# Attention values projected with tokens on partitions, in a hybrid decoder layer on one core

## The chip, the cores and the metric

The program runs on one core of a Trainium2 chip. The metric is the device time of one execution in microseconds; less is better. Three runs of the kernel before took 854.75, 854.88 and 855.74 us, median 854.88.

## The reference

One layer of a decoder over 256 prompt tokens and 8 requests with 8 new tokens each (64 sample tokens, 320 in all). Everything is float32. The residual stream (320 x 2048) goes through one wide projection whose columns feed three branches; the part that matters here is the sparse attention:

```python
z = jnp.einsum('btd,dn->btn', h, w)              # 2048 -> 8272 columns
aq, ak, av, ag, iq, ik, iw, bq, bf, bi, bg, mq, mg = jnp.split(z, cuts, axis=-1)
sc = sum_h iw[h] * relu(iq[h] . ik)              # 16 index heads of 64
sel = top_k(sc, 64 for the prompt, 256 for a sample request)
p = softmax(aq . ak[sel] / sqrt(128));  a_out = p @ av[sel]     # 8 heads of 128
```

A sample request attends over 2048 cached keys and values, which lie in 16 pages of 128 tokens, named by a page table, and over its 8 new ones. The second branch is a gated linear recurrence (HGRN2, 4 heads), the third attends to 256 memory tokens. Each branch is multiplied by a gate, the three are concatenated, projected by `w_out` and normalised. New keys, values, index keys and states are outputs too.

## The kernel before

**Precision.** The fast format of TensorE (`F32R`) holds a rounded float32, so each large product is made in three passes: a tensor is split into a high part and a rest (`xh`, `xl` for the tokens, `wh`, `wl` for a weight), and `xh*wh + xl*wh + xh*wl` is accumulated in PSUM.

**Projection.** The input projection goes column block by column block in the order of `PROJECTIONS`: first the index keys and two index heads, then `queries` (index and attention queries), `ak`, `av`, and then HGRN and gates, with the memory's projection between. For nearly all of it the weights are stationary: a 128 x 128 piece of the weights is loaded and the 320 tokens stream past, so the result has its features on partitions and the tokens along the row (tile `pj`, two PSUM banks that alternate). An entry of `wspec` is one 512 KB load of weights (ring `wr`, 3 buffers), prepared in two halves by a cast on ScalarE (`wh`) and a subtraction on VectorE or GpSimd (`wl`); `pe_quantum` runs an entry in four quanta of 6 products. When a block has all of its 16 slices, its evacuation stands in `pending` until PSUM holds the result and tiles of ring `t` are free. `ev_ak` turns a head of keys by the rotary tables (a shuffle and a product on VectorE read the bank); `ev_av` copies a head of values, 128 features x 320 tokens, and stores it to `vT`.

**Attention values.** The product of probabilities and values needs tokens on partitions. `attn_values` therefore transposes each head on TensorE: three transposes of 128 columns, a copy to `avn` (prompt) and one to `avS` (the 64 sample tokens), then three products with the transposed probabilities `probs(h)`. `attn_scores` makes those: scores, exponent and division in two `t` tiles `P0`, `P1`, three transposes, and a copy into space of `cat` that is free at that time.

**Pages.** Keys and values of the cache come in units: for a pair of requests and two pages each, 4 loads of 512 KB (`load_pages`, queue of SP). Tags `pg` (5 buffers) and `S` (3) hold them. A key unit is 16 products of 32 stationary columns by 256, a value unit 8 by 512, spread over the four 32-column groups of TensorE, so that four run side by side. Units go in the order of `PAGES` and, where both are loaded, two at a time; a key unit needs the queries, a value unit the softmax `soft(p)` of its pair, which needs the mask of the sample's top-k.

**Order.** All engines run their instructions in order, and one program writes that order out ahead of time. `Plan` keeps an estimated clock for every engine, with a price for each operation (`Engine.cost`), a time for each transfer and a time from which each tile can be read. The main loop at the end moves with TensorE: it starts loads (`loads`), prepares weights, issues evacuations, resumes the generators in `bg` (`background`) whose wants are met, and then gives TensorE a unit if `units_now` says so, or the next quantum if `half_ready` says so; if neither is ready, the estimated time moves on. After a unit, `join_visit` may add work that asked for a shared visit (`need(..., visit=...)`): such work waits up to `visit` us of the plan for one before it goes alone. The plan decides the order only; on the chip semaphores do.

**Other names.** `idx_load` brings the index keys, 32 KB pieces through GpSimd's indirect loads and SP, into a tile of 128 x 2048 for each pair of requests (`st["ci", p]`); `idx_sample` scores them; `idxdone` marks its end and is followed by `topk_sample`, 32 rounds of an 8-fold maximum and a replacement on VectorE. `masks` brings constants. Ring `bp` has two tiles of 4 KB a partition, shared by the index queries, the constants, the top-k's running count, HGRN and the memory queries (`pad_queries`). `VACC` is the sum of a pair's value units in PSUM bank `va`. `new_keys(p)` makes the scores of a pair against the new keys.

Of the kernel before, what the change touches and what calls it, by code (L numbers as in the profile page):

```python
# [47 lines left out]
IDLE = 3.0  # L48
LOOK = 3
# [96 lines left out]
class Engine:  # L146
# [41 lines left out]
    def cost(self, op, outs, ins, n):  # L188
        if self.name == "PE":
# [8 lines left out]
            if a.dtype == F32R:  # L198
                return turn + 0.0087 + n * 0.0004325
# [29 lines left out]
def hymba_step(ctx: ExitStack, tc: tile.TileContext, I, O):  # L229
# [223 lines left out]
    def pad_queries():  # L453
        yield from wait(("mq", 0))
# [70 lines left out]
    def add_block(kind, i):  # L525
# [3 lines left out]
        elif kind == "mem":  # L529
            for k in range(16):  # L530
                wspec.append(dict(kind="mem", k=k, n=1024, nq=2, src=I["wm"][:, k, :]))
        else:
            base, ev = {"iq": (32, ev_iq), "aq": (0, ev_aq), "ak": (8, ev_ak), "av": (16, ev_av), "mq": (56, ev_mq),
# [128 lines left out]
    def page_tag(n):  # L662
# [3 lines left out]
        if (len(PG) - len(in_s) + ("q" in st) + ("more" in st) + ci_live(0) < BUFS["pg"]  # L666
                and plan.slot_free("pg", BUFS["pg"]) <= plan.now + 0.2):
            return "pg"
# [53 lines left out]
    def unit(n):  # L722
# [21 lines left out]
        elif kind == "V":  # L744
            if u == 0:
                VACC[p] = PS([128, 512], "va")
            for j in range(2):
# [31 lines left out]
    def unit_ready(n):  # L779
        kind, p, u = punits[n]  # L780
        if any((n, b) not in PG or plan.avail(PG[n, b]) > plan.now for b in range(2)):
            return False
# [4 lines left out]
        if kind == "V":  # L787
            return ("soft", p) in done and plan.avail(PTt[p]) <= plan.now and (u < 7 or "attn" in done) and (
# [8 lines left out]
    def loaded(n):  # L797
        return all((n, b) in PG and plan.avail(PG[n, b]) <= plan.now for b in range(2))
# [38 lines left out]
    def ci_live(k):  # L837
        return sum([0, 1, 1, 1][p] == k and ("ci", p) in st for p in range(4))

    def idx_load():  # L840
# [3 lines left out]
        for sp in range(2):  # L844
            for p in (2 * sp, 2 * sp + 1):
                st["ci", p] = x = new([128, PAST], "S" if p else "pg")
                plan.pinned.add(x.tensor.name)
                plan.split.add(x.tensor.name)
            for c in range(2):
                for f in (1, 0):  # L850
                    for p in (2 * sp, 2 * sp + 1):
                        parts = []
                        j = 8 * f + 4 * c
# [6 lines left out]
                        for i in range(2):  # L860
                            x = st["ci", p][:, 128 * (j + i):128 * (j + i) + 128]
# [3 lines left out]
                        for i in range(2, 4):  # L865
                            for b in range(2):
                                yield from idle("SP", 0.5)
                                x = st["ci", p][64 * b:64 * b + 64, 128 * (j + i):128 * (j + i) + 128]
# [48 lines left out]
    def idx_sample():  # L917
# [77 lines left out]
        def stack(k):  # L995

            sp, c, f, a = steps[k]
            raw = st["ci", 2 * sp + a][:, 1024 * f + 512 * c:1024 * f + 512 * c + 512]
# [5 lines left out]
            if (c, f) == (1, 0):  # L1004
                plan.pinned.discard(st["ci", 2 * sp + a].tensor.name)
                del st["ci", 2 * sp + a]
# [142 lines left out]
    def attn_scores():  # L1149
        yield from wait("pbias", "idxdone")  # L1150
        for h in range(8):
            yield from wait(("aq", h), ("ak", h))
            yield from room(2)
# [4 lines left out]
            P0, P1, s8 = T(128), T(256), T8()  # L1158
# [17 lines left out]
            ACT.copy(probs(h), pt)  # L1176
            free(P0, P1)
            done.add(("probs", h))

    def attn_values():  # L1180
        for h in range(8):
            yield from wait(("probs", h), ("av", h))
            yield need(AV[h])
            avn = new([128, 2, 128], "avn")
            ps = PS([128, 3, 128])
            for i in range(2):
                PE.transpose(ps[:, i, :], AV[h][:, 128 * i:128 * i + 128], ident)
            PE.transpose(ps[:, 2, :], AV[h][:, 192:320], ident)
            ACT.copy(avn, ps[:, 0:2, :])
            ACT.copy(avS[64:128, 128 * h:128 * h + 128], ps[64:128, 2, :])  # L1190
            free(AV.pop(h))
            pts = probs(h)
            yield need(pts, avn)
            po = PS([128, 256])
            PE.matmul(po[:, 0:128], avn[:, 0, :], pts[:, 0:128], start=True, stop=True)
            PE.matmul(po[:, 128:256], avn[:, 0, :], pts[:, 128:256], start=True, stop=False)
            PE.matmul(po[:, 128:256], avn[:, 1, :], pts[:, 256:384], start=False, stop=True)
            cat_put(h, "p", slice(0, 256), po, ACT.copy)
        done.add("attn")

    def new_keys(p):
# [4 lines left out]
        yield need(akS, st["qpad"], visit=VISIT_WAIT)  # L1206
# [55 lines left out]
    def extract(p):  # L1262
# [3 lines left out]
        for i in range(2):  # L1266
            ACT.activation(o[i], VACC[p][:, 256 * i:256 * i + 256], AF.Copy, scale=RS[p][:, 1:2])
        del VACC[p], PTt[p]
# [96 lines left out]
    def hgrn():  # L1365
        lb, olb = lbt[:, 8:12], lbt[:, 12:16]
        yield from wait("idxdone", "pbias", "masks")
        for h in range(4):
# [4 lines left out]
            late_q = new([128, 2, 48], "kN")  # L1373
            yield from room(2, spare=spare)
# [270 lines left out]
    def half_ready(i, q):  # L1645
# [40 lines left out]
    def pe_quantum(i, q):  # L1686
# [12 lines left out]
        if s["kind"] == "T":  # L1699
# [14 lines left out]
            if s["k0"] + s["nk"] == 16 and last:  # L1714
                pending.append((s["evac"], pj.pop(s["evac"]), 3))
                if i == last_T:
                    done.add("lastT")
        elif s["kind"] == "mem":
# [86 lines left out]
    def ln_load(m):  # L1805
# [8 lines left out]
        if m == 0:  # L1814
            x = new([128, 2, 8, 6], "avn")
# [171 lines left out]
    def masks():  # L1987
        yield from wait("idxdone")
        yield from room(2, "bp")
        cm = [new([128, 1024], "bp"), new([128, 1024], "bp")]  # L1990
        SP.dma_start(lbt[:, 0:8], I["lb"])
        SP.dma_start(ngt, I["ng"])
        SP.dma_start(cm[0], I["cm"][:, 0:1024])
        SP.dma_start(cm[1], I["cm"][:, 1024:2048])
        yield need(*cm, lbt, ngt)
        ACT.copy(cu8, cm[0][:, 0:304])
# [275 lines left out]
```

## Time and profile before

| | |
|---|---|
| median of three runs | 854.88 us (854.75 to 855.74) |
| profiled execution | 854.57 us, span 852.8 us |
| TensorE busy, products | 843.1 us |
| weight loads of TensorE | 718.0 us |
| VectorE, ScalarE, GpSimd busy | 553.9, 422.3, 326.0 us |
| moved by DMA | 266.49 MB, mean 312 GB/s |

The span runs from the first instruction to the last; the profiled execution's own time has 1.8 us around it. TensorE's products are pipelined: one is still running when the next starts, so a row's duration is longer than its share of the engine, and what a product costs in a stream is the distance between starts. Nearly every operation has line 157, the helper that records all of them; rows are told apart by their tiles, output to the left of the arrow: `pj<-xh,wh` is a product of the input projection, `kv<-pg,qpad` one of a key unit, `va<-pg,PT` one of a value unit, `mB<-ident,t` a transpose. A product of true float32 operands stands as two records.

### The profile page before, as it was taken

To read this page: it belongs to the slowest core of one execution; us is meant where nothing else is said; L and a number is where in the kernel's file an instruction comes from. 1 tells how busy PE (TensorE), PEld (TensorE's weight loads), DVE (VectorE), ACT (ScalarE), POOL (GpSimd) and SP (SyncE) were. 2 spreads that over 40 slices of the span, in tenths; PEclk is the share of its full clock that TensorE was granted. 3 is DMA by queue.
4 is the path that set the end of the run, shared out by engine and by line. 5 is a ranking of instruction groups with operands and counts; after the bars stand their busy time and mean duration, and the time that the engine had idled before them with its cause. 6 is when DMAs were issued, how large, how long until landed. Compare 5 with 4: busy or idle time off the path is not lost.

```text
span 852.8 us, 19150 instructions
## 1 busy us (share of the span) xinstructions
PE 843.1 (99%) x6892; PEld 718.0 (84%) x6892; DVE 553.9 (65%) x1100; ACT 422.3 (50%) x908; POOL 326.0 (38%) x333
## 2 busy tenths in 40 slices
PE   9999999999999999999999999999999999999996
PEld 8999999877889898878778788787887889888885
DVE  7788897744897898654474556557545343953655
ACT  6454565553555543634544554554444353744432
POOL 0677562564634445331142214333311110714424
PEclk9999999999999999999999999999999999999998
DMA  9567456889999999999989999999999988756633
GB/s 342 172 189 228 156 172 251 279 307 411 376 389 397 335 327 359 398 360 403 389 330 409 408 353 389 401 397 377 347 409 400 364 324 291 272 171 199 195 99 123
DMA packets 83216, 266.49 MB, mean 312 GB/s; under 512 B 10481, under 2 KB 21170, under 8 KB 82482
## 3 DMA queue, kind: packets, MB, share of 16 engines
q1 hardware_dynamic: 82098, 263.18, 83.6%
q0 software_dynamic: 1024, 2.10, 0.8%
q8 instruction: 54, 0.88, 0.4%
q14 instruction: 40, 0.33, 0.1%
HBM read 256.50 MB, written 8.73 MB: 311 GB/s over the span
## 4 chain that ended last, share of the span: by engine, by line
PE 98%; DMA 1%; DVE 0%; SPq 0%; ACT 0%; DVEq 0%; issue 0%
PE pj L157 57%; PE mB L157 13%; PE va L157 10%; PE mA L157 10%; PE kv L157 8%; DMA S<-in_first 1%; DVE pg L157 0%; SPq L157 0%; ACT xh L157 0%; ACT PT L157 0%; DVE s L157 0%; DVEq L2258 0%; DVE avn L157 0%
## 5 line engine op out<-in xcount | busy, mean ns | idle before, releaser
L157 ACT CAST wh<-wr 128x512 fp32r<-128x512 f32 x334 | 205.0, 621 | 243.5 <-PE pj L157 183.9
L157 PE MATMUL pj<-xh,wh 128*128 128x320 f32 (+1 forms) x992 | 313.6, 316 | 0.0
L157 PE MATMUL pj<-xh,wl 128*128 128x320 f32 (+1 forms) x992 | 303.9, 306 | 0.0
L157 PE MATMUL pj<-xl,wh 128*128 128x320 f32 (+1 forms) x992 | 303.8, 306 | 0.0
L157 DVE TENSOR_TENSOR wl<-wr,wh 128x512 fp32r<-128x512 f32 x222 | 172.7, 785 | 181.9 <-ACT wh L157 166.5
L157 POOL TENSOR_TENSOR wl<-wr,wh 128x512 fp32r<-128x512 f32 x112 | 151.0, 1357 | 240.2 <-ACT wh L157 222.7
L157 PEld LDWEIGHTS pj<-xh,wh 128*128 128x128 f32 x992 | 186.7, 188 | 16.0 <-issue 12.5
L157 PEld LDWEIGHTS pj<-xl,wh 128*128 128x128 f32 x992 | 186.8, 188 | 1.3
L157 PEld LDWEIGHTS pj<-xh,wl 128*128 128x128 f32 x992 | 186.6, 188 | 0.0
L157 POOL TENSOR_TENSOR t<-t,t 128x256 f32<-128x256 f32 (+3 forms) x53 | 46.2, 873 | 119.5 <-ACT t L157 60.0
L157 PE MATMUL va<-pg,PT 128*32 128x512 f32 x456 | 58.4, 595 | 0.0
L157 PE MATMUL kv<-pg,qpad 128*32 128x256 f32 (+1 forms) x916 | 57.5, 380 | 0.0
L157 PEld LDWEIGHTS kv<-pg,qpad 128*32 128x32 f32 (+1 forms) x916 | 30.8, 110 | 20.4 <-issue 1.3
L157 PEld LDWEIGHTS va<-pg,PT 128*32 128x32 f32 x456 | 14.6, 109 | 30.4 <-issue 28.1
L157 DVE MAX8 PT<-PT 128x8 f32<-128x1032 f32 x32 | 39.5, 1234 | 0.5
L157 DVE MATCH_REPLACE8 PT<-PT 128x1032 f32<-128x1032 f32 x32 | 39.0, 1218 | 0.0
L157 POOL DMA_INDIRECT S<-in_ci,row x24 | 25.5, 1064 | 20.0 <-DVE row L157 10.6
L157 PE MATMUL mB<-t,wh 128*128 128x256 f32 x128 | 24.5, 289 | 0.0
L157 POOL TENSOR_TENSOR bp<-t,bp 128x128 f32<-128x128 f32 (+1 forms) x17 | 10.7, 627 | 36.0 <-ACT bp L157 36.0
L157 DVE TENSOR_TENSOR cat<-S,cat 64x512 fp32r<-64x512 f32 x24 | 19.5, 813 | 6.9 <-ACT cat L157 6.4
L157 POOL TENSOR_TENSOR t<-t,tabm 128x320 f32<-128x320 f32 x16 | 14.5, 908 | 24.4 <-DVE t L157 24.2
L157 POOL TENSOR_TENSOR xl<-cat,xh 128x256 fp32r<-128x256 f32 x12 | 12.5, 1061 | 24.8 <-ACT xh L157 24.8
(430 smaller groups left out, 1355.0 us busy)
## 6 DMA issues: line engine op xcount, KB each, us to landing
wr<-in_wt SPq DMA_DIRECT2D x124, 512.0 KB
pg<-in_ck SPq DMA_DIRECT2D x114, 512.0 KB
pg<-in_cv SPq DMA_DIRECT2D x114, 512.0 KB
wr<-in_wo SPq DMA_DIRECT2D x36, 512.0 KB
wr<-in_wm SPq DMA_DIRECT2D x16, 512.0 KB
S<-in_ck SPq DMA_DIRECT2D x14, 512.0 KB
S<-in_cv SPq DMA_DIRECT2D x14, 512.0 KB
pg<-in_cXV SPq DMA_DIRECT2D x8, 512.0 KB
```

What stands on the lines that cost most here:

```text
L157: res = f(*a, **k)
```

## The change

1. **Values with tokens on partitions.** The block `av` becomes 16 entries of kind `av`: two chunks of 512 columns, each over 8 loads of two slices. The tokens are stationary: 128 prompt tokens (`m` 0), 128 more (`m` 1), and, for `m` 2, the sample tokens' high and low parts side by side in one 128-wide weight `xS`, which `sample_columns` copies together into both `bp` tiles after `idxdone`. 512 columns of weights stream past; three passes for `m` 0 and 1, two for `m` 2. The accumulators are both `pj` banks and `va`; a chunk starts when nothing is pending and one `pj` bank and `va` are free. `ev_av` copies, adds the two halves of the sample part into `avS`, and stores rows of tokens (output `v`). `attn_values` has no transposes left.
2. **Scores in place.** `attn_scores` writes its probabilities to `probs(h)` at once, without two `t` tiles and without waiting for room for them.
3. **Value units** wait for the sample values of both chunks, since `va` is shared, and `VACC` is pinned until it is read.
4. **Index keys** lie by halves of the pages, a tile for each half of two pairs, and a tile is given back after its half.
5. **Pages** are requested from entry 28 on (38 before), and a unit counts as loaded 2 us of the plan after its planned landing (`PAGE_LAG`).
6. **Visits.** `join_visit` asks whether the wants are met 0.4 us before the plan's end of TensorE's work; `new_keys` waits up to 18 us for a visit (9 before).
7. **Smaller ones.** A weight load is asked for 0.6 us after its buffer comes free in the plan (up to 1 us ahead of that, before); `masks` runs after the index queries with one load into a `pg` tile; `pad_queries` waits for HGRN's last head to have its `bp` tiles; the plan's price of a fast product is n/2400 + 0.0133 us.

```diff
-    def ev_av(h):
-        def f(ps):
-            AV[h] = T()
-            ACT.copy(AV[h], ps)
-            store(O["vT"][h], AV[h])
-            done.add(("av", h))
+    def ev_av(n, m):
+        def f(acc):
+            ps, = acc
+            if m == 2:
+                c = slice(512 * n, 512 * n + 512)
+                ACT.copy(avS[64:128, c], ps[64:128])
+                DVE.tensor_add(avS[64:128, c], avS[64:128, c], ps[0:64])
+                store(O["v"][256:320, c], avS[64:128, c])
+                done.add(("avs", n))
+                return
+            for j in range(2):
+                AV[m, 2 * n + j] = t = T(256)
+                (DVE.tensor_copy if m else ACT.copy)(t, ps[:, 256 * j:256 * j + 256])
+                store(O["v"][128 * m:128 * m + 128, 512 * n + 256 * j:512 * n + 256 * j + 256], t)
+            if m:
+                done.update(("av", h) for h in range(4 * n, 4 * n + 4))
...
+        elif kind == "av":
+            if i % 4 == 0:
+                for k in range(0, 16, 2):
+                    wspec.append(dict(kind="av", nch=i // 4, k=k, n=1024, nq=4,
+                                      src=I["wv"][i // 4, :, k:k + 2, :].rearrange("p a c -> p (a c)")))
...
-            yield from room(2)
             yield need(AQ[h], AK[h], pbias)
...
-            P0, P1, s8 = T(128), T(256), T8()
+            s8, pts = T8(), probs(h)
+            P0, P1 = pts[:, 0:128], pts[:, 128:384]
...
+    def sample_columns():
+        yield from wait("idxdone")
+        yield from room(2, "bp")
+        xS = [new([128, 8, 128], "bp", F32R) for _ in range(2)]
+        for i in range(2):
+            for x, c in ((xh, 0), (xl, 64)):
+                (DVE.tensor_copy if c else ACT.copy)(xS[i][:, :, c:c + 64], x[:, 8 * i:8 * i + 8, 256:320])
...
-            yield need(AV[h])
-            avn = new([128, 2, 128], "avn")
-            ps = PS([128, 3, 128])
-            for i in range(2):
-                PE.transpose(ps[:, i, :], AV[h][:, 128 * i:128 * i + 128], ident)
-            PE.transpose(ps[:, 2, :], AV[h][:, 192:320], ident)
-            ACT.copy(avn, ps[:, 0:2, :])
-            ACT.copy(avS[64:128, 128 * h:128 * h + 128], ps[64:128, 2, :])
...
-        yield need(akS, st["qpad"], visit=VISIT_WAIT)
+        yield need(akS, st["qpad"], visit=2 * VISIT_WAIT)
...
+        if s["kind"] == "av":
+            return s["k"] or q or "xS" in st and plan.avail(st["xS"][1]) <= plan.now and not pending and max(plan.slot_free("pj", 2), plan.slot_free("va", 1)) <= plan.now
...
+        elif s["kind"] == "av":
+            n, K = s["nch"], s["k"] + q // 2
+            ms = ((0, 2), (1,)) if n == K == 0 else ((0,), (1, 2))
+            for m in ms[q % 2]:
+                if K == 0:
+                    pj["av", m] = PS([128, 512], "va" if m == 2 else "pj")
+                ps = pj["av", m]
+                t = slice(128 * m, 128 * m + 128)
+                xS = st["xS"][K // 8][:, 128 * (K % 8):128 * (K % 8) + 128]
+                xs = [(xS, hi), (xS, lo)] if m == 2 else \
+                    [(xh[:, K, t], hi), (xl[:, K, t], hi), (xh[:, K, t], lo)]
+                for x, w in xs:
+                    PE.matmul(ps, x, w, start=K == 0 and x is xs[0][0] and w is hi, stop=K == 15 and w is lo)
...
-            if e[1] and e[1][3] and met(e[1]):
+            if e[1] and e[1][3] and met(e[1], max(plan.now, plan.t["PE"] - 0.4)):
...
-            if nw < len(wspec) and nw < half + 5 and plan.slot_free("wr", 3) <= plan.now + 1 and nw - nprep < 3 \
+            if nw < len(wspec) and nw < half + 5 and plan.slot_free("wr", 3) <= plan.now + (-0.6) and nw - nprep < 3 \
...
-            if half > 38 and n < len(punits) and page_tag(n) and plan.t["DMA"] < plan.now + 4:
+            if half > 28 and n < len(punits) and page_tag(n) and plan.t["DMA"] < plan.now + 4:
```

More of the change, by code (lines that the diff above doesn't have):

```diff
@@ L48 @@
 IDLE = 3.0
+PAGE_LAG = 2.0
 LOOK = 3
@@ L453, in pad_queries @@
     def pad_queries():
-        yield from wait(("mq", 0))
+        yield from wait(("mq", 0), ("hgrn", 3))
         yield from room(1, "bp")
@@ L746, in unit @@
                 VACC[p] = PS([128, 512], "va")
+                plan.pinned.add(VACC[p].tensor.name)
             for j in range(2):
@@ L780, in unit_ready @@
         kind, p, u = punits[n]
-        if any((n, b) not in PG or plan.avail(PG[n, b]) > plan.now for b in range(2)):
+        if not loaded(n):
             return False
@@ L787, in unit_ready @@
         if kind == "V":
-            return ("soft", p) in done and plan.avail(PTt[p]) <= plan.now and (u < 7 or "attn" in done) and (
+            return ("soft", p) in done and ("avs", 1) in done and plan.avail(PTt[p]) <= plan.now and (u < 7 or "attn" in done) and (
                 u or plan.slot_free("va", 1) <= plan.now)
@@ L797, in loaded @@
     def loaded(n):
-        return all((n, b) in PG and plan.avail(PG[n, b]) <= plan.now for b in range(2))
+        return all((n, b) in PG and plan.avail(PG[n, b]) + PAGE_LAG <= plan.now for b in range(2))
     def units_now(n):
@@ L837, in ci_live @@
     def ci_live(k):
-        return sum([0, 1, 1, 1][p] == k and ("ci", p) in st for p in range(4))
+        return sum((2 * sp + c != 1) == k and ("ci", sp, c) in st for sp in range(2) for c in range(2))
     def idx_load():
@@ L844, in idx_load @@
         for sp in range(2):
[L845 to L848, printed above, removed]
             for c in range(2):
+                st["ci", sp, c] = t2 = new([128, PAST], "S" if 2 * sp + c != 1 else "pg")
+                plan.pinned.add(t2.tensor.name)
+                plan.split.add(t2.tensor.name)
                 for f in (1, 0):
@@ L1175, in attn_scores @@
             PE.transpose(pt[:, 256:384], P1[:, 128:256], ident)
-            ACT.copy(probs(h), pt)
-            free(P0, P1)
+            ACT.copy(pts, pt)
             done.add(("probs", h))
+    def sample_columns():
[5 more added lines that the diff above has]
+                (DVE.tensor_copy if c else ACT.copy)(xS[i][:, :, c:c + 64], x[:, 8 * i:8 * i + 8, 256:320])
+        st["xS"] = [x.rearrange("p k t -> p (k t)") for x in xS]
     def attn_values():
@@ L1373, in hgrn @@
             late_q = new([128, 2, 48], "kN")
+            done.add(("hgrn", h))
             yield from room(2, spare=spare)
@@ L1717, in pe_quantum @@
                     done.add("lastT")
+        elif s["kind"] == "av":
[11 more added lines that the diff above has]
+                    PE.matmul(ps, x, w, start=K == 0 and x is xs[0][0] and w is hi, stop=K == 15 and w is lo)
+                if n == 1 and K == 15 and m == 2:
+                    free(*st["xS"])
+                if K == 15:
+                    f = ev_av(n, m)
+                    if m == 2:
+                        other_bank.append(f)
+                    pending.append((f, [pj.pop(("av", m))], 0 if m == 2 else 2))
         elif s["kind"] == "mem":
@@ L1987, in masks @@
     def masks():
-        yield from wait("idxdone")
-        yield from room(2, "bp")
-        cm = [new([128, 1024], "bp"), new([128, 1024], "bp")]
+        yield from wait(("iq", 3))
+        st["cm"] = cm = new([128, 2048], "pg")
         SP.dma_start(lbt[:, 0:8], I["lb"])
         SP.dma_start(ngt, I["ng"])
[L1993 to L1996, printed above, removed]
-        ACT.copy(emat.rearrange("p a b c d -> p (a b c d)"), cm[1])
-        free(*cm)
+        SP.dma_start(cm, I["cm"])
+        yield need(cm, lbt, ngt, ps=0)
+        yield from idle("ACT", 0.3)
+        ACT.copy(cu8, cm[:, 0:304])
+        ACT.copy(emat.rearrange("p a b c d -> p (a b c d)"), cm[:, 1024:2048])
+        del st["cm"]
         DVE.tensor_scalar(ngt, ngt, -0.5, None, op0=OP.mult)
@@ L2036, in hymba_step, with met @@
     asked = {}
-    def met(want):
+    def met(want, now=None):
         deps, nps, lag, _ = want
-        return all(plan.avail(a) + lag <= plan.now for a in deps) and (not nps or n_free("mA") + n_free("mB") >= nps)
+        return all(plan.avail(a) + lag <= (now or plan.now) for a in deps) and (not nps or n_free("mA") + n_free("mB") >= nps)
     def resume(e):
```

51 lines of the change are left out of this document (28 added, 23 removed).

## Prediction

> **What bounds the kernel now.** I read the page first, for the shares of the engines and the chain that ended last, then what TensorE waited for, then single stretches of the timeline around the value projection.
>
> ```profile
> span 852.8 us, 19150 instructions
> ...
> PE 843.1 (99%) x6892; PEld 718.0 (84%) x6892; DVE 553.9 (65%) x1100; ACT 422.3 (50%) x908; POOL 326.0 (38%) x333
> ...
> PEclk9999999999999999999999999999999999999998
> ...
> PE 98%; DMA 1%; DVE 0%; SPq 0%; ACT 0%; DVEq 0%; issue 0%
> ```
>
> The chain is TensorE from end to end, at the full granted clock. A busy share alone could hide pipelining, so the waits of TensorE are the second view (us in total, times, longest):
>
> ```profile
> PE kv L1947 <- DVE t L157: 1.1, 1, 1.1
> PE va L157 <- ACT PT L157: 0.6, 1, 0.6
> ```
>
> Two waits, 1.7 us, both at the start, before the first projection is under way. So nothing that only makes data come sooner can gain more than about these, and the change touches neither. The time moves only if TensorE has fewer columns to stream, fewer changes of shape, or new waits. The profiled execution took 854.57 us around its span of 852.8; the median of the three runs is 854.88, 0.31 us above it. I sum against the span and carry the difference over to the median unchanged. About 0.2% (1.7 us) is what a measurement of this kernel can tell from no change.
>
> **The projection of the values.** Cadences are read from uninterrupted stretches of the chain of waits (start, us, what):
>
> ```profile
> 596.92 8.80 PE pj L157 x60
> ...
> 828.64 9.52 PE mB L157 x42
> ```
>
> Sixty 320-column products take 8.80 us, 146.7 ns each; forty-two 512-column ones 9.52 us, 226.7 ns each. Before, the values are 8 heads x 16 slices x 3 passes = 384 products of 320 columns: 384 x 0.1467 = 56.3 us. After, tokens are the stationary side: 2 column chunks x 16 slices x (3 + 3 + 2) = 256 products of 512 columns: 256 x 0.2267 = 58.0 us. The 64 sample tokens save a pass because their high and low parts lie side by side in one 128-wide weight, yet the columns streamed rise from 384 x 320 = 122,880 to 256 x 512 = 131,072. This half of the edit costs **+1.7 us**; fewer instructions only win part of it back.
>
> What it removes are the transposes that bring a head's values to tokens on partitions, three a head, 24 in all:
>
> ```profile
> 224.08 0.31 PE L157 MATMUL pj<-xh,wl 128*128 128x320 f32 x1
> 224.23 0.49 PE L157 MATMUL mB<-ident,t 128*128 128x128 f32 x3
> 224.55 0.82 PE L157 MATMUL mA<-t,t 128*128 128x128 f32 x4
> 225.02 0.49 PE L157 MATMUL pj<-xh,wh 128*128 128x320 f32 x1
> 225.36 0.31 PE L157 MATMUL pj<-xl,wh 128*128 128x320 f32 x1
> ```
>
> Three 128-column transposes (here of probabilities, same shape) occupy 224.55 - 224.23 = 0.32 us, 0.107 each: 24 x 0.107 = **-2.6 us**. The products of probabilities and values stay. Net of the edit: **-0.9 us**, and this is the only part of the diff that changes how much TensorE streams. Their eight visits go too. On return the first 320-column product holds 225.36 - 225.02 = 0.34 us instead of 0.147; whether these 0.19 us are a price of the visit or only the end of its last product, the rows can't say. Eight visits are worth 0 to 1.5 us; since 224.23 came on the cadence, 0.15 after the product ahead of it, I take **-0.2**, near nothing.
>
> Here a rule of the Trainium skill speaks against the change. Its page "TensorE: Matmul & The Clock Gate", section "Back-to-back issue gap", puts a lone stream at columns / 2.4 + 2.5 ns. An estimate by that page is 135.8 and 215.8 ns, so +3.1 us in place of +1.7, and a net of +0.5. The rows above show 13.4 ns over columns / 2.4 at both widths, not 2.5, so I keep -0.9.
>
> **Changes of shape.** A visit of 32-column products between the projection's 128-column ones costs something on both sides (the timeline of TensorE):
>
> ```profile
> 363.57 0.31 PE L157 MATMUL pj<-xh,wl 128*128 128x320 f32 x1
> 363.81 0.62 PE L157 MATMUL va<-pg,PT 128*32 128x512 f32 x2
> ...
> 367.38 0.41 PE L157 MATMUL pj<-xh,wh 128*128 128x320 f32 x1
> 367.64 0.30 PE L157 MATMUL pj<-xl,wh 128*128 128x320 f32 x1
> ```
>
> Going in, 0.24 us against the cadence of 0.147; coming out, 0.26 against 0.147: 0.21 us a visit. Two kinds of 32-column work could share a page unit's visit and stand alone now: the scores against the new keys (one visit here with two pairs) and the HGRN score blocks (four of them; first and last from the chain).
>
> ```profile
> 247.85 0.65 PE L157 MATMUL mB<-akS,qpad 128*32 128x64 f32 x32
> 248.32 0.63 PE L157 MATMUL mA<-akS,qpad 128*32 128x64 f32 x32
> ```
>
> ```profile
> 389.01 1.41 PE mB L157 x93
> ...
> 635.52 1.41 PE mB L157 x93
> ```
>
> `join_visit` now asks whether the operands are ready 0.4 us before the unit on TensorE ends, and `new_keys` waits twice as long for a chance. At most 5 x 0.21 = 1.05 us goes; at least nothing, or 0.3 us is lost if a joined visit then waits for data. I take **-0.8 us**. Who waits for the longer patience: `soft`, which stands behind the mask anyway.
>
> **Two new waits.** A chunk of values starts only when nothing is pending and PSUM is free: three accumulators (two of `pj`, one of `va`) instead of two that alternate. At the first chunk the last key head must be evacuated. The VectorE timeline of before shows that evacuation inside the top-k's chain:
>
> ```profile
> 222.39 1.24 DVE L157 MAX8 PT<-PT 128x8 f32<-128x1032 f32 x1
> ...
> 225.98 0.52 DVE L157 STREAM_SHUFFLE t<-pj 128x320 f32<-128x320 f32 x1
> 226.39 0.48 DVE L157 TENSOR_TENSOR t<-pj,tabm 128x320 f32<-128x320 f32 x1
> 226.78 1.23 DVE L157 MAX8 PT<-PT 128x8 f32<-128x1032 f32 x1
> ```
>
> Shuffle and product hold the bank 0.8 us (225.98 to 226.78) after waiting for up to a pair of selections (two of about 1.2 us). The first quantum, `ms` = (0, 2), needs only one `pj` bank and runs 5 x 0.227 = 1.1 us before the second is touched. Exposed: 0 to 2.2 us. Freed tiles could delay that evacuation further, but scores now write to `cat` and no longer hold two tiles of `t`. At the second chunk `va` must be emptied by a copy and an addition like this one:
>
> ```profile
> 206.68 0.69 DVE L157 TENSOR_TENSOR PT<-PT,va 128x512 f32<-128x512 f32 x1 [3.00 <-PE va L157]
> ```
>
> With the ScalarE copy taken as long, that is 1.4 us after a queue of 0 to 2.5 us on VectorE: 1.4 to 3.9 us. Whatever else is ready goes first: a pair of key units takes 3.59 us, and four heads of values become ready at that moment.
>
> ```profile
> 231.53 3.59 PE kv L157 x64
> ```
>
> So both waits together cost 0 to 6.1 us. I take **+0.8**, near the lower end, because covering work was found without a gap across this whole stretch of before (100% busy below). If no unit is ready, it is the upper half.
>
> **Edits taken at nothing.** The DMA share by stage, and the longest waits of SP's queue:
>
> ```profile
> 94.00:128.00 34.00, 34.00 (x228) 33.30 (x227) 32.72 (x84) 21.69 (x43) 18.35 (x21) 1.00 0.48 152
> 220.00:311.00 91.00, 91.00 (x915) 80.91 (x914) 80.98 (x134) 49.34 (x128) 43.00 (x35) 1.00 0.98 368
> ```
>
> ```profile
> SPq L157 <- DVE wl L157: 154.2, 79, 6.3
> SPq L157 <- POOL wl L157: 129.3, 54, 6.5
> ```
>
> Pages from weight 28 on instead of 38 fill transfers that run at 0.48 of capacity from 94 to 128 us; key units then start earlier, but TensorE was busy with something else there, so only the order moves. Weight loads asked 1.6 us later in the plan take away some of the 283 us for which SP stood on a weight buffer with page requests behind it; the transfers are 98% busy behind that, so what this frees is order, not bytes. Cost if a weight then lands late: a gap before a quantum, which before has none of. The 2 us of page slack delays a unit by two quanta of projection, which fill the place. Index keys by halves of the pages move the same bytes and give the first buffer back half-way. The mask constants go as one 1 MB load, before the pages, on SP and into a `pg` tile; nothing behind it waits yet. `pad_queries` waits for HGRN's last head and stays ahead of its units. The stores carry the same bytes.
>
> The values keep both `bp` tiles until they are done, and the top-k wants one for its running count:
>
> ```profile
> 320.80 2.31 DVE L157 TENSOR_TENSOR_SCAN bp<-one,PT 128x1032 f32<-128x1032 f32 x1
> ```
>
> ```profile
> L157 SPq DMA_DIRECT2D out_vT<-t x8: 348/360/1175, 235.1 to 313.7; - x8
> ```
>
> The last head of values is stored at 313.7, seven us before the count; the new order ends about there too. The first value unit (363.81 above) is 50 us behind, so `("avs", 1)` does not delay it.
>
> **Sum.** -0.9 - 0.2 - 0.8 + 0.8 = -1.1 us: span 851.7, and 854.88 - 1.1 = **853.8** by the median. That is less than the 1.7 us that can be told apart.
>
> **Rivals.** *Everything hides and joins*: -0.9 - 1.05, both chunk waits covered, and the eight removed visits worth between nothing and their full 1.5 us: -2.0 to -3.4, so 852.9 to 851.4; with a third of the 1.5 it is 852.4. For it: TensorE never idled in this stretch, and the same fillers are still there. Against: the first chunk's bank is behind a VectorE that is 81 of 91 us busy. Chance 0.34.
>
> *The chunk waits decide* (the other side): at the second chunk no unit and no head is ready, because key units, requested earlier, are already used up or stand in their slack. The place is the two starts of a chunk, the price up to 6.1 us: -1.9 + 6.1 = +4.2, or 859.1. It decides from an uncovered 3.6 us on (-1.9 + 3.6 = +1.7, 856.6); half-way between is 857.8. For it: the VectorE rows above. Against: the 3.59 us units and the score visits that have to be run somewhere. Chance 0.23.
>
> The Trainium skill's same page, Part 1 on the clock gate, adds that an idle window of about 3.4 us halves TensorE's clock until it is busy again. No row here shows it, the granted clock is 9 tenths or more up to the last slice; it would add an estimated 1.7 us to this case.
>
> *It does not do what it says*: no visit is joined, and earlier pages change nothing. Then -0.9 - 0.2 + 0.8 = -0.3, 854.6, inside the forecast's own case.
>
> **Chances.** Within 0.2%, 853.2 to 856.6, the forecast's case with the one without joins: 0.43; faster 0.34; slower 0.23. The range leaves out the outer parts of both rivals, about a tenth each: 852.0 (a little over half of the 1.5 us) to 857.8.
>
> **What would show it.** In the changed profile: 256 products of 512 columns with stationary `xh`, `xl` or `bp`, at 0.227 us each; 24 transposes of `t` fewer; fewer lone visits with `akS` and with 91 to 93 small products; TensorE still 98 to 99% busy. Gaps, if any, stand right before the first product of `va` in the value projection, and before the first 512-column `pj` product of its second chunk. I am wrong if the cadence at 512 columns with stationary tokens is not 0.227, if TensorE shows waits elsewhere (a late weight or page), or if the difference lies after the last unit, where nothing was changed.

## The result, and the profile after

The kernel after took 862.9 us (median of 4 runs, 861.12 to 864.38) where the kernel before, beside it, took 854.9 (854.75 to 855.74): a ratio of 1.0091, 95% interval 1.0070 to 1.0111. It is 8.0 us slower; the forecast was 1.1 us faster. The profiled execution of after is its fastest run, 861.12 us, so its trace explains 6.6 of the 8.0 us. From its page:

```profile
span 859.4 us, 18833 instructions
...
PE 846.0 (98%) x6740; PEld 708.2 (82%) x6740; DVE 554.8 (65%) x1106; ACT 420.3 (49%) x894; POOL 333.4 (39%) x335
...
PEclk9999999999999999999999999999999999999998
...
PE 34%; DMA 2%; DVE 1%; ACT 0%; issue 0%; DVEq 0%; ACTq 0%
```

TensorE still looks full, 98% after 99%. The chain says otherwise: it was 98% TensorE, and now it can be followed through TensorE for only 34%, with a DMA of weights in it. The span grew by 6.6 us and TensorE's busy time by 2.9, so 3.7 us are idle time, and the rest is hidden in "busy", because a product's modelled end runs past the next start. Two views find it, what the products waited for and what the weight loads (PEld) waited for (us in total, times, longest):

```profile
PE mA L158 <- DVE s L158: 1.6, 2, 1.2
PE kv L1992 <- DVE t L158: 1.1, 1, 1.1
PE pj L158 <- DVE t L158: 1.0, 1, 1.0
PE pj L158 <- DVE wl L158: 0.9, 2, 0.6
```

```profile
PEld pj L158 <- ACT t L158: 4.2, 6, 0.8
...
PEld pj L158 <- ACT wh L158: 2.3, 4, 1.2
PEld mA L158 <- DVE s L158: 1.6, 1, 1.6
PEld pj L158 <- DVE wl L158: 1.6, 3, 0.8
```

`wh` and `wl` are freshly split weights, `t` is the split memory operand, `s` an operand of HGRN's scores. Before showed two waits of products, 1.7 us in all. To place the loss I took, for every product, the distance to the next start less what its shape takes in an unbroken stream (146.7 ns at 320 columns, 226.7 at 512, and so on). This excess sums to 10.9 us before and 18.0 after, +7.1; the streams themselves are 0.9 us shorter, and the last product starts 6.2 us later. Of the +7.1, 3.2 lie at 60 to 80 us, 1.9 at 520 to 560, and the rest is scattered in smaller pieces. The table of stretches shows the two places as idle TensorE (the first number is the length, the second TensorE's busy time; the last three are granted clock, DMA share and GB/s). Before:

```profile
60.00:80.00 20.00, 20.00 (x160) 19.49 (x159) 17.87 (x37) 8.76 (x16) 16.07 (x17) 1.00 0.66 203
...
500.00:580.00 80.00, 80.00 (x797) 64.24 (x796) 48.55 (x108) 44.27 (x97) 28.97 (x35) 1.00 1.00 383
```

After:

```profile
60.00:80.00 20.00, 17.95 (x138) 16.39 (x137) 13.96 (x35) 10.75 (x19) 12.37 (x14) 1.00 0.62 204
...
500.00:580.00 80.00, 78.58 (x762) 65.41 (x761) 50.43 (x108) 42.47 (x94) 26.47 (x30) 1.00 0.95 362
```

Neither place is in the value projection, which runs from 228.5 to 312 us. Its cadence, from the timeline of TensorE after (start, us):

```profile
263.80 0.39 PE L158 MATMUL pj<-wh,xh 128*128 128x512 f32 x1
...
265.39 0.39 PE L158 MATMUL va<-wl,bp 128*128 128x512 f32 x1
```

Seven distances in 1.59 us are 0.227 each, as forecast. At the start of the second chunk, where the rival saw up to 6.1 us, a key unit and four heads of values fill the place, and the whole stretch has no idle TensorE:

```profile
270.05 0.39 PE L158 MATMUL va<-wl,bp 128*128 128x512 f32 x1
270.37 1.93 PE L158 MATMUL kv<-pg,qpad 128*32 128x256 f32 x32
272.23 0.94 PE L158 MATMUL mA<-cat,t 128*128 128x128 f32 x6
```

```profile
220.00:270.00 50.00, 50.00 (x446) 38.91 (x445) 39.40 (x70) 23.47 (x59) 26.32 (x22) 1.00 0.98 374
270.00:313.00 43.00, 43.00 (x311) 32.93 (x314) 36.26 (x55) 19.52 (x44) 21.12 (x17) 1.00 0.92 336
```

**The place at 63 to 69 us.** SP's queue after, between two loads of weights:

```profile
50.05 0.54 SPq L158 DMA_DIRECT2D wr<-in_wt  x1
...
51.59 0.42 SPq L158 DMA_DIRECT2D pg<-in_cm  x1
52.53 2.99 SPq L158 DMA_DIRECT2D S<-in_ci  x3
55.62 0.53 SPq L158 DMA_DIRECT2D wr<-in_wt  x1
```

The 1 MB of mask constants (`cm`), two small ones and three pieces of index keys stand between them; before asked for weights at 49.90, 51.51 and 55.03. (The masks follow the index queries' block 3, not the last of them; before asked for the constants at 220.48 us only.) ScalarE then waits for a weight and has the masks' own work between its casts:

```profile
62.53 0.62 ACT L158 CAST wh<-wr 128x512 fp32r<-128x512 f32 x1 [5.24 <-DMA wr<-in_wt]
...
63.40 1.04 ACT L158 CAST emat<-pg 128x1024 bf16<-128x1024 f32 x1
...
64.98 1.28 ACT L185 ACT_TABLE_LOAD   x1
```

and TensorE's weight loads wait for the casts:

```profile
68.21 0.19 PEld L158 LDWEIGHTS pj<-xh,wh 128*128 128x128 f32 x1 [1.22 <-ACT wh L158]
69.34 0.19 PEld L158 LDWEIGHTS pj<-xh,wl 128*128 128x128 f32 x1 [0.84 <-DVE wl L158]
```

**The place at 520 to 560 us.** Here four weights of the memory projection (`wm`) between 540 and 560 us land 0.5 to 4.0 us after ScalarE is ready to cast them (before: two, 0.7 and 1.7 us); the DMA engines are busy without a pause from 516 us on, and were not just ahead of it. After:

```profile
508.00:512.00 4.00, 4.00 (x60) 2.86 (x62) 1.82 (x2) 2.98 (x7) 2.11 (x2) 1.00 0.38 152
512.00:516.00 4.00, 4.00 (x73) 3.48 (x66) 3.97 (x14) 1.92 (x5) 0.00 (x0) 1.00 0.48 105
540.00:550.00 10.00, 10.00 (x104) 7.46 (x103) 4.68 (x8) 3.96 (x11) 4.12 (x7) 1.00 1.04 401
```

```profile
544.04 0.62 ACT L158 CAST wh<-wr 128x512 fp32r<-128x512 f32 x1 [4.00 <-DMA wr<-in_wm]
...
558.94 0.62 ACT L158 CAST wh<-wr 128x512 fp32r<-128x512 f32 x1 [2.79 <-DMA wr<-in_wm]
```

Before has no such hole:

```profile
508.00:512.00 4.00, 4.00 (x31) 3.99 (x30) 4.00 (x8) 1.35 (x4) 1.38 (x1) 1.00 0.80 292
512.00:516.00 4.00, 4.00 (x36) 3.60 (x38) 3.97 (x13) 1.77 (x4) 2.90 (x3) 1.00 1.02 404
```

From 508 to 516 us after leaves 4 x 0.62 + 4 x 0.52 = 4.6 us of DMA time unused, before 0.8.

### The profile page after: what moved, and what is told of

Read it like the earlier page. It is cut to its first block, busy times and chain, and to the rows that moved or that the text cites. A ratio compares the mean times of both kernels' runs of the same rounds, so it can differ in the third digit from the quotient of the medians.

```text
span 859.4 us, 18833 instructions
## 1 busy us (share of the span) xinstructions
PE 846.0 (98%) x6740; PEld 708.2 (82%) x6740; DVE 554.8 (65%) x1106; ACT 420.3 (49%) x894; POOL 333.4 (39%) x335
## 2 busy tenths in 40 slices
DMA packets 83231, 266.47 MB, mean 310 GB/s; under 512 B 10497, under 2 KB 21186, under 8 KB 82370
## 5 line engine op out<-in xcount | busy, mean ns | idle before, releaser
L158 PE MATMUL pj<-xh,wh 128*128 128x320 f32 (+1 forms) x864 | 272.9, 316 | 1.1 <-DVE t L158 1.0
L158 PE MATMUL pj<-xh,wl 128*128 128x320 f32 (+1 forms) x864 | 264.7, 306 | 1.0 <-DVE wl L158 0.9
L158 PE MATMUL pj<-xl,wh 128*128 128x320 f32 (+1 forms) x864 | 264.4, 306 | 0.0
L158 POOL TENSOR_TENSOR wl<-wr,wh 128x512 fp32r<-128x512 f32 x121 | 164.2, 1362 | 251.3 <-ACT wh L158 205.6
L158 PEld LDWEIGHTS pj<-xh,wh 128*128 128x128 f32 x864 | 162.6, 188 | 18.4 <-issue 11.4
L158 PEld LDWEIGHTS pj<-xh,wl 128*128 128x128 f32 x864 | 162.6, 188 | 1.6 <-DVE wl L158 1.6
L158 PEld LDWEIGHTS pj<-xl,wh 128*128 128x128 f32 x864 | 162.8, 188 | 1.3
L158 POOL DMA_INDIRECT S<-in_ci,row x24 | 26.0, 1083 | 18.6 <-DVE row L158 10.9
L158 PE MATMUL pj<-wh,xh 128*128 128x512 f32 x64 | 26.8, 418 | 0.0
L158 PE MATMUL pj<-wh,xl 128*128 128x512 f32 x64 | 25.0, 391 | 0.0
L158 PE MATMUL pj<-wl,xh 128*128 128x512 f32 x64 | 25.0, 391 | 0.0
```

Source lines behind the costliest of these rows:

```text
L158: res = f(*a, **k)
```

## The experiments

Eighteen kernels ran. Theories as the expectations name them: W, the weight requests come too late; M, the early masks; T, any newly written order costs some us; U, each edit has a price of its own; L, operands land later than the plan counts on, and room would repair it; D, transfer time that is lost ahead of a stretch with full DMA engines can't be made up. Medians stand beside the before of the same chip, 854.8 to 855.1.

**Weight requests, masks, both.** On after:

```diff
-plan.slot_free("wr", 3) <= plan.now + (-0.6)
+plan.slot_free("wr", 3) <= plan.now + 1          # e1, e3
-        yield from wait(("iq", 3))
+        yield from wait(("iq", 6))               # e2, e3: masks
```

> The changed kernel with one number put back: a weight load is asked for when its buffer comes free within 1 us of the plan, as before, not 0.6 us after that. Theory W (weights land late because they are asked for 1.6 us later, and this is most of the 7 us of new gaps): 856 to 858, the gaps between 520 and 560 us (1.9 us more than before) gone, and part of the 3.2 us at 63 to 69 us. Theory M (the early mask constants, on SP's queue and on ScalarE, make the gap at 63 to 69 us): at least 859, that gap stays at about 3 us. Rival C (the starts of the value chunks, as in the prediction's slower case): no change from 862.9.

> The changed kernel with the mask constants started after index query 6 instead of 3, some 35 us later, nothing else. Theory M: the gap at 63 to 69 us is gone, about 3 us faster than 862.9, so near 859.5, and the rest of the gaps stays. Theory W: the weight that landed at 62.5 us is late all the same, at most 1 us is won. Rival C: no change.

> Both edits of the two runs before together. W and M as two separate causes: their gains add up, TensorE's gaps are back near those of the kernel before, and the time is 854 to 855.5, that is the forecast's -0.9 us of columns and nothing else. Rival C: 860 or more, with gaps at the starts of the value chunks.

Measured: 862.6 (861.52 to 862.96), 861.5 (860.30 to 863.89) and 860.4 us (859.44 to 861.74), ratios 1.0087 (1.0073 to 1.0101), 1.0079 (1.0065 to 1.0094) and 1.0064 (1.0051 to 1.0078). W alone is not the cause: both places stay, with an excess of 2.9 us and 2.5. M is right about the place. After, against the kernel with later masks:

```profile
64.00:68.00 4.00, 3.06 (x22) 2.65 (x22) 2.31 (x11) 3.97 (x8) 0.13 (x1) 1.00 0.54 179
68.00:72.00 4.00, 3.13 (x24) 2.96 (x25) 4.00 (x8) 1.18 (x3) 3.02 (x4) 1.00 0.30 107
```

```profile
64.00:68.00 4.00, 4.00 (x36) 4.00 (x35) 4.00 (x7) 1.14 (x2) 3.62 (x4) 1.00 0.73 239
68.00:72.00 4.00, 4.00 (x35) 3.87 (x36) 2.72 (x6) 1.82 (x4) 3.51 (x5) 1.00 0.75 218
```

In this kernel the constants are asked for at 75.98 us, 24 us later than in after and not 35. All four kernels of the whole set with later masks (e2, e3, e12, e16) keep TensorE busy for the full 20 us from 60 to 80; the eight with early masks, whatever else is changed, for 17.8 to 19.4. But 3.2 us won there became 1.4 in the median: the new order has an excess of 4.2 us at 80 to 160 us, where after has 1.2. Both together leave 5.4 us unexplained, with 2.5 at 520 to 560 us.

**Single edits put on before.**

```diff
-plan.slot_free("wr", 3) <= plan.now + 1
+plan.slot_free("wr", 3) <= plan.now + (-0.6)     # e4
-                return turn + 0.0087 + n * 0.0004325
+                return turn + 0.0133 + n / 2400  # e5: the plan's price, no work
-            if half > 38 and ... page_tag(n)
+            if half > 28 and ... page_tag(n)     # e6
-        yield need(akS, st["qpad"], visit=VISIT_WAIT)
+        yield need(akS, st["qpad"], visit=2 * VISIT_WAIT)   # e7, with
+            ... met(e[1], max(plan.now, plan.t["PE"] - 0.4)) # join_visit
```

> The kernel before with weight loads asked for 1.6 us later (0.6 us after the buffer is free in the plan, not up to 1 us ahead), nothing else. Theory W: slower by 2 to 4 us, 857 to 859, with gaps before projection or memory products that wait for a cast or a subtraction of a weight. If the late request only frees SP, as the prediction had it: 854.9 within 1 us.

> The kernel before with the changed kernel's price for a fast product in its plan (n/2400 + 0.0133 us: half a nanosecond less for 320 columns, 3.5 less for 512), nothing else. No work is changed, only which of two ready things the plan takes first here and there. Theory T (the order of before fits the chip closely, and any other order that the plan writes meets operands a few us later than planned): 857 to 860, with gaps of 0.3 to 3 us at places that have nothing to do with the edit. Theory W+M (two causes, late weights and early masks): 854.9 within 1 us.

> The kernel before with pages requested from entry 28 on, nothing else. The prediction took this at nothing. Theory P (pages ahead of weights in SP's queue at 94 to 128 us make the weights late): slower by 2 us or more with gaps there. Theory T: slower by 2 to 5 us with gaps anywhere later. W+M: 854.9 within 1 us.

> The kernel before with the visits alone: join_visit asks 0.4 us ahead of the planned end of TensorE's work, new_keys waits up to 18 us. The prediction gave it -0.8 us: 854.1. Theory J (a joined visit waits for operands that the plan had ready): slower by 1 to 3 us, the gaps before HGRN's 32-column products (1.4 us with the changed kernel) and before new-key products. Theory T: slower by 2 to 5 us with gaps elsewhere too.

Measured: 859.4 (858.56 to 860.83), 859.0 (857.99 to 860.18), 857.1 (856.36 to 857.91) and 861.2 us (860.05 to 861.84); ratios 1.0049 (1.0035 to 1.0063), 1.0047 (1.0033 to 1.0060), 1.0025 (1.0016 to 1.0034), 1.0066 (1.0053 to 1.0080). Edits that I had priced at nothing or as a gain cost 2 to 6 us, even one that changes only the plan's arithmetic. Where it goes differs, and no large gap stands where W, P or J had it. With pages from entry 28 on one unit waits 1.9 us for a page. With late weight requests the second of two key units waits for its page in a stretch of full DMA engines (weight loads and stretches of that kernel):

```profile
233.93 1.47 PEld L157 LDWEIGHTS kv<-pg,qpad 128*32 128x32 f32 x28 [2.82 <-issue]
```

```profile
230.00:236.00 6.00, 3.63 (x57) 1.95 (x50) 5.00 (x12) 3.77 (x12) 2.49 (x2) 1.00 0.99 389
```

With joined visits the DMA engines have a hole at 504 to 512 us, and 20 us on a key unit waits 3.69 us for its page; from 533 to 538 us the granted clock is 0.50:

```profile
504.00:508.00 4.00, 4.00 (x54) 3.00 (x56) 1.45 (x2) 3.29 (x7) 1.80 (x2) 1.00 0.51 204
508.00:512.00 4.00, 4.00 (x78) 3.34 (x68) 3.96 (x13) 1.61 (x5) 0.31 (x1) 1.00 0.43 66
```

```profile
533.01 0.18 PEld L157 LDWEIGHTS kv<-S,qpad 128*32 128x32 f32 x3 [3.69 <-issue]
```

**The values with the old settings.** After with weight requests, start of the pages, page slack, patience and joining put back (`PAGE_LAG = 0.0`, and the lines above the other way round):

> The changed kernel with five numbers of its plan put back (page request 38, no page slack, weight request 1 us ahead, visits as before): the values with tokens on partitions, the scores in place, index keys by halves, early masks and the price of a product remain. If the projection itself is worth what the prediction said and the numbers are the cause: 854 to 856. Rival C (chunk starts): 859 or more with gaps at the two starts of a chunk. Theory T: 858 to 863, gaps scattered, none at the chunk starts.

868.8 us (866.59 to 869.70), ratio 1.0155 (1.0141 to 1.0169). Putting the settings back costs 6 us. That the settings are worth this much on the new values isn't shown: the next runs move the time by 5.6 us without any change of work. Late pages hold 4.2 us here.

**Is it any new order?** The plan's price alone, on after put back to the old one, and on before raised by 0.3 ns:

```diff
-                return turn + 0.0133 + n / 2400          # e9, on after
+                return turn + 0.0087 + n * 0.0004325
-                return turn + 0.0087 + n * 0.0004325     # e10, on before
+                return turn + 0.0090 + n * 0.0004325
```

> The kernel after with only the plan's price of a product put back to that of before; no work is changed, 4136 lines of the listing of TensorE's products differ. Theory T (an order that the plan has newly written costs some us wherever operands happen to land late, whatever the edit): another time than 862.9, anywhere from 858 to 868, and the gaps of TensorE sit in other places than at 63 and 520 to 560 us. Rival U (each edit has a price of its own, the plan's price has none but by a better fit): 862.4 to 863.4, gaps in the same places.

> The kernel before with the plan's price of a fast fp32 product raised by 0.3 ns (0.0087 to 0.0090 us); no work is changed, and the new price is no better fit to the rows. The order is the old one up to about 370 us and another one behind that (2348 lines of the listing of products differ). Theory T: 856.5 to 861, with one to three new gaps of 0.7 to 3 us behind 370 us. Rival U: 854.3 to 855.3, since neither work nor a setting is changed.

868.5 us (866.84 to 869.87), ratio 1.0158 (1.0144 to 1.0171), and 854.9 us (854.49 to 855.88), ratio 1.0004 (0.9995 to 1.0013). The first is above T's range by half a microsecond; the second refutes T as stated: a new order behind 370 us that costs nothing. U falls by the first. But e9 is no clean case for T's places either: the masks' place stays (TensorE is busy for 17.97 of the 20 us from 60 to 80), and the largest new gap is at 606 us. A new order can cost nothing (e10) or 5.6 us (e9 beside after), and what decides had to be found.

**Room for the landing.** The plan's landing time of a load on after later by 1.5, 1 and 3 us (e11, e17, e18); 0.8 us between a cast and its use on the kernel of e3 (e12); 1.5 us on the kernel of e3 (e16):

```diff
-            self.w[self.key(out)] = end + 1.0
+            self.w[self.key(out)] = end + 2.5    # e11, e16; e17: 2.0; e18: 4.0
-        if ... plan.avail(WL[i][p])) > plan.now:
+        if ... plan.avail(WL[i][p])) + 0.8 > plan.now:   # e12
```

> The kernel after with only the plan's landing time of a load put 1.5 us later (end of transfer + 1.0 to + 2.5 us). Theory L (the gaps come because the plan counts on weights and pages earlier than they land, and room between the landing and the use removes them): 855 to 858, weight-load waits on wh, wl, t and s below 2 us in sum. Theory T (it is just another new order): 859 to 867, gaps as large as in after (sum of excess 16 to 22 us), in other places.

> The kernel after with the weight request at +1 us and the masks behind six index queries (860.4 us so far), and a half of a weight is taken 0.8 us after the plan has its cast done. Theory L: 855 to 857.5, the waits of weight loads for wh and wl gone (each of those seen was 0.2 to 1.2 us). Theory T: 858.5 to 864.

> The kernel after with the landing of a load counted 1.5 us later, the weight request at +1 us and the masks behind six index queries. If room for landing is what after lacks and the masks are its other cost: 854 to 856.5, below the 858.0 of the landing alone, no gap above 0.5 us at 63 to 69 us and none above 1 us at 520 to 560. If each new order falls as chance has it: 857 to 862.

> The kernel after with the landing of a load counted 1.0 us later instead of 1.5. Room is the cause: 858 to 861, between after (862.9) and the landing at 1.5 us (858.0). The order falls as chance has it: anywhere from 857 to 869, and each sizable gap behind a hole of the DMA engines (a stretch of 4 us at a share below 0.6 shortly ahead of it).

> The kernel after with the landing counted 3.0 us later. Room is the cause: 855 to 858, weight-load waits on cast weights below 1 us in sum. Chance of the order: anywhere from 857 to 869.

Measured: 858.0 (857.29 to 858.36), 860.5 (859.49 to 860.73), 862.3 (861.86 to 863.59), 862.0 (860.99 to 862.71) and 878.6 us (876.07 to 881.16); ratios 1.0034 (1.0021 to 1.0048), 1.0065 (1.0051 to 1.0079), 1.0085 (1.0071 to 1.0099), 1.0080 (1.0066 to 1.0094) and 1.0279 (1.0259 to 1.0299). With 0, 1, 1.5 and 3 us of room the kernel takes 862.9, 862.0, 858.0 and 878.6: no order in it, and L falls, though the 858.0 alone lay in its range; the 878.6 lies far outside both ranges and was not traced. In e17 the largest gap, 2.3 us at 733 us, stands behind 12 us of full DMA engines (716 to 728 us) and not behind a hole, as was expected there. The 858.0 is the best of after's family and still 3.1 us behind before. In e16 the early gap is gone and 520 to 560 is at before's level, yet TensorE stands at 592 us, for an operand that ScalarE copies late. From its timeline and its table of stretches:

```profile
596.31 0.90 PE L158 MATMUL mB<-ident,t 128*128 128x128 f32 x3 [3.38 <-ACT t L158]
```

```profile
596.00:600.00 4.00, 3.69 (x15) 3.69 (x16) 2.57 (x3) 1.62 (x4) 1.28 (x1) 0.50 1.01 385
```

The same wait stands in e9, 3.39 us at 606 us. It is no late transfer: ScalarE itself waits there 2.46 us for VectorE.

**Transfers alone, the order held.** To separate D from the order, one transfer was changed behind the plan's back, so that the rows of TensorE, VectorE and ScalarE keep their order. On before three loads' worth of bytes more, behind the second or the fourth store of a state; on after one store of a state less (that part of the output isn't written):

```diff
                 SP.dma_start(dst, src)
+                if dst.tensor.name == "out_ss":
+                    n_ss[0] += 1
+                    if n_ss[0] == 2:             # e13; e14: 4
+                        for r, c in ((0, 0), (0, 1024), (128, 0)):
+                            nc.sync.dma_start(O["y"][r:r + 128, c:c + 1024], ...)   # 512 KB each, from xh
```

> The kernel before, with the order of TensorE, VectorE and ScalarE as it was row for row, and three more transfers of 512 KB (from the prompt's tokens to an output that is written again later) behind the store of a state at 502.6 us. By the rows' 400 GB/s they take 3.9 us. Theory D (the DMA engines are full from 512 to 570 us, so lost transfer time is paid by TensorE): 856 to 859, with new gaps of 1.5 to 4 us at 515 to 575 us. Rival (the gaps come of the order, DMA has room): 854.5 to 855.3.

> The same three transfers of 512 KB behind the store of a state at 670.7 us, ahead of the stretch 700 to 720 us, where the DMA engines are busy for 0.60 and 0.76 of the time; the order of the compute engines is again that of before. Theory D: at most 1 us more than before (854.5 to 856), since the queue has room soon behind it. A rival by which any foreign transfer of this size costs its 3.9 us: 857 to 859.

> The kernel after with the order of the compute engines as it was, without the store of one state (512 KB) at 513.3 us; that part of the output is not written. 512 KB at 400 GB/s are 1.3 us. Theory D: the gap of 2.8 us at 520 to 560 us falls by 0.8 to 1.5 us, 861.4 to 862.1 (862.9 before this edit). Rival: the gap stays at 2.8, 862.5 to 863.3.

Measured: 860.2 (859.78 to 861.28), 855.4 (855.08 to 856.09) and 862.0 us (860.04 to 863.36); ratios 1.0063 (1.0049 to 1.0077), 1.0004 (0.9995 to 1.0013), 1.0086 (1.0072 to 1.0100). The same 1.5 MB cost 5.1 us at 502 us and 0.4 at 671, which can't be told from nothing. Row for row, TensorE in the first kernel falls 4.6 us behind before between 511 and 521 us and keeps that to the end. There:

```profile
516.00:520.00 4.00, 1.88 (x32) 0.87 (x24) 3.90 (x9) 1.19 (x4) 1.34 (x2) 1.00 1.03 402
...
520.00:530.00 10.00, 9.52 (x70) 7.82 (x71) 2.15 (x7) 3.60 (x8) 1.24 (x2) 0.83 1.03 406
```

```profile
PE kv L157 <- DMA pg<-in_ck: 2.6, 1, 2.6
```

3.9 us of transfer come out as 2.6 us of idle TensorE for a page, and 1.7 more (10 us at a clock of 0.83): above my range by the clock, which I had not counted. Taking a store away changed the time too little to tell (862.0 beside 862.9, on other chips), but its place answered. Row for row, TensorE gains 1.4 us on after between 528 and 561 us; elsewhere these two executions drift apart by up to 0.7. After, then after without the store:

```profile
560.00:570.00 10.00, 9.06 (x166) 5.95 (x167) 6.08 (x21) 5.26 (x12) 3.10 (x4) 1.00 0.99 374
```

```profile
560.00:570.00 10.00, 9.92 (x172) 6.65 (x172) 5.78 (x20) 5.55 (x14) 2.97 (x5) 1.00 0.99 369
```

The excess at 520 to 560 us fell from 2.8 to 1.6 us, 1.2 us for a store of 1.3. D holds for this stretch, by the order held, in both directions; the second rests on one execution of each kernel.

The other traces of after's family agree, in orders of their own. e1, e2, e3, e9 and e12 leave 4.1 to 4.4 us of DMA time unused from 508 to 516 us, as after does, and their excess at 520 to 560 is 0.8 to 1.8 us above that of before. e11, e16 and e17 leave 0.6 to 0.8 us, and theirs is at most 0.1 above. e8 and e18 leave as little and lose 2.4 and 2.6 us all the same: a hole there is not the only way to lose time in this stretch.

## Why the prediction was wrong

*Cadence and transposes, -0.9 us*: right. The 256 products run at 0.227 us, and the streams sum to 0.9 us less. The Trainium skill's formula for a lone product, in the section "Back-to-back issue gap" of "TensorE: Matmul & The Clock Gate", would by the prediction's estimate have made it +0.5; here too the rows show 13 ns over columns / 2.4, not 2.5. The -0.2 for the visits that go was not measured by itself.

*The chunk waits, +0.8, and their rival up to 6.1*: no wait there. The fillers I named, a key unit and four heads, stood ready.

*Joined visits, -0.8*: in part. Before had three lone visits of the scores against new keys (247.9, 309.6 and 501.7 us; the prediction counted one), and in after all three stand behind page units (240.6, 312.5 and 509.6 us), while HGRN's four still stand alone. At the prediction's 0.21 us a visit that is an estimated 0.6 us. But the gain can't be had by itself: on before the edit costs 6.4 us, with a hole in the transfers, a 3.2 us gap of TensorE and the clock behind it at half.

*"Edits taken at nothing"* is the step that failed. Of the masks I wrote "nothing behind it waits yet": the next weight load behind them in SP's queue went out 4.1 us later than before, casts of weights on ScalarE stood behind the masks' own work, and TensorE lost 3.2 us, as e2 shows. Of the weight requests and pages I wrote that what they free "is order, not bytes", and looked for harm only in a single late weight. The row that I quoted, a DMA share of 0.98 from 220 to 311 us (500 to 580 us has 1.00), said more: where the DMA engines are full, a hole ahead of the stretch can become debt that TensorE pays within it; from 520 to 560 us it paid 1.9 us for the 3.8 us that after left unused beyond before's. The bytes were the same (266.47 MB after 266.49); when they were asked for was not. And the first argument, that two waits of TensorE are all that data could cost or bring, bounds only the gain. A kernel at 99% has its slack on one side: a new order can take away little waiting and can add much, though it need not (e10 added none).

What is shown: the early masks as the cause of the first place (e2, in a new order, with the rows of waits beside it and the same answer in e3, e12 and e16; what the queue, the 1 MB and ScalarE's work each add isn't told apart); the debt of transfers as cause of the second (e13 and e15, with the order held). The hole itself at 508 to 516 us is seen, and not traced to one of the edits: at 512.92 us SP takes up a weight's load after 8.4 us for its buffer. The weight requests and the masks are not its cause alone, since it stays without them (e1, e2, e3). With joined visits alone, before has one too (e7), and e8, where joining is among the five settings put back, has none; but e11, which keeps them, has none either, so the visits remain a guess. The scattered rest, some 2 us in after, has no cause by experiment, and the 3.4 us gaps of e9 and e16 show another kind, a chain between ScalarE and VectorE. Masks alone, the page slack alone, the index halves alone, and the values alone on before were not tried.

## What to carry to other kernels

Where a program writes the order of all engines out ahead of time and one engine is full, an edit's price isn't only its work: the new order has to be measured, and more than one of them, before the edit is judged; here a change of 0.3 to 3.5 ns in the plan's price moved the time by 0 to 5.6 us. Before calling a moved load free, look at the DMA share of the 50 us behind it: 3.9 us of transfer more cost 5.1 us ahead of a full stretch here, and no more than noise ahead of one with room. To tell a cause from the luck of the order, change one transfer without telling the planner.

## What the runs showed of the hardware

A gap of TensorE can cost more than its length, because the granted clock halves behind some gaps. After 3.05 us without a weight load (e13) it was 0.83 over the next 10 us, and in e16, after 3.4 us without a product, 0.50 over the next 4. The length of one gap doesn't decide it: after 2.82 us without a weight load (e4) the clock stayed at 1.00, and after 2.76 us (e17) it fell to 0.50. In e9 it fell at 69.8 us, where no wait of a weight load since 60 us was longer than 1.22 us, but products filled only 2.32 of the 4 us from 66 to 70. e17, then e9:

```profile
734.71:738.13 3.42, 3.42 (x10) 2.50 (x9) 3.35 (x7) 1.07 (x3) 2.02 (x2) 0.50 0.50 147
```

```profile
70.00:73.00 3.00, 3.00 (x16) 3.00 (x16) 3.00 (x7) 0.62 (x1) 1.79 (x3) 0.50 0.53 178
```

By the clock's records these stretches at half last 3.4 us (e9, e13, e17) or 6.8 us (e7, e16), so each costs up to an estimated 1.7 or 3.4 us on top of the gap. The Trainium skill's page "TensorE: Matmul & The Clock Gate", Part 1, puts the idle window at about 3.4 us and the clock behind it at half; the half agrees, and here shorter gaps were enough.

The other surprise is the landing time of a 512 KB load, which differs between a full and a half-empty stretch. The page of after (us to landing at the end):

```profile
wr<-in_wo SPq DMA_DIRECT2D x36, 512.0 KB, 4.4
...
wr<-in_wm SPq DMA_DIRECT2D x16, 512.0 KB, 7.0
```

The output's weights, most of them loaded where the DMA engines are busy for 0.40 to 0.77 of the time (720 to 840 us), take 4.4 us, the memory's in the full stretch 7.0.
